# Scales of MLP weights from a 2-norm on ScalarE, halves of an exponential buffer split, two modulation steps a period instead of three: a two-layer diffusion backbone on one core

## The chip, the cores and the metric

One Trainium2 chip, one of its cores. The time is device microseconds of one execution; the kernel before took 2903.8 us in the median of 3 runs (2901.84 to 2909.9). The kernel is written with a tile framework: the program names tiles and operations, and a planner that works with an estimated timeline sets semaphores, buffers and the order of each engine's queue at compile time. On the chip every engine works through its queue in that order.

## The reference, cut to what matters

```python
for layer in range(2):
    mp, ms = ada_mod(c_ctx, w_ada[layer], b_ada[layer]), ada_mod(c, w_ada[layer], b_ada[layer])
    h = modulate(rmsnorm(x, norm1[layer]), m[0], m[1])
    # layer 0: mixer A (windowed attention with sink) and mixer B (differential attention); layer 1: RG-LRU
    x = x + m[2] * mixer(h)
    h = modulate(rmsnorm(x, norm2[layer]), m[3], m[4])
    x = x + m[5] * (square(relu(h @ w_mlp1[layer])) @ w_mlp2[layer])
y = rmsnorm(x, final_norm)

# ada_mod: silu(c) @ w + b, split in six; w is 1024 x 6144
# diff_attention: w = softmax(q1 k1 * SCALE) - lam * softmax(q2 k2 * SCALE); w @ v
```

There are 1,024 latent and 128 context tokens, width 1,024, an MLP width of 4,096, and everything is fp32.

## The kernel before, in words

TensorE works on fp16 pairs. Each fp32 operand becomes hi + lo after multiplication by a power of two, and a product is three matmuls. The power of two comes from a bound of the operand: it has to be large enough for precision and small enough that nothing overflows.

**The MLP** (`mlp`, L474). The weights come in quarters of 1,024 KB (class `Quad`, L2103): 16 upper ones (kind U, 256 columns of w_mlp1) and 16 lower ones (kind D, 512 x 512 of w_mlp2) a layer, 64 in all, in two staging buffers `st` of 128x2048. The products go by a scheme with seven block products in place of eight, so a quarter is split twice: as it is, then after sums of its blocks. A quarter goes through these steps, spread over the products of the two quarters before it (`pieces` in `mlp`):

- `load`: a DMA from SP's queue into `st`;
- `peak` (L2113): VectorE takes the largest absolute value of each partition (`rowmax`, L109, or the reduction at L2120 for the two halves of a lower quarter, each with its own scale), TensorE spreads these over the partitions (`across`, L115: a matmul with the column repeated as weights and the identity as the moving operand), and VectorE takes the maximum again (L123);
- `bits` (L2123): VectorE makes the scale in one-column instructions (`pow2s`, L94 to L103, and others);
- `prepare`: ScalarE writes hi (L2142) and VectorE lo (L2143), in halves of 128x1024; GpSimd forms the block sums in place (L2163 to L2166); hi and lo again. After the last lo the staging buffer is free for the next load.

Meanwhile ScalarE applies relu and square (L650, L651) to the upper products, GpSimd and VectorE form sums of the activations (L639 to L642, L569), ScalarE and VectorE or GpSimd split these (L151, L152), and VectorE adds finished lower products to X (L713). The products (L520) turn through six PSUM accumulators; TensorE starts one when VectorE or ScalarE has emptied it. The prompt's 128 tokens have small tiles of their own: `gt` (two buffers, fp32 128x256) for its activations.

**The attention** (`attention`, L871). Units of mixer A and of mixer B, 36 each, are started, exponentiated, combined, split, transposed by DMA and multiplied with V. What a unit does when is written in tables of offsets in periods (`PLAN_A`, `PLAN_B`, `PLAN_C` for the last nine units of mixer B); all events are sorted by these due times, and the program is written out in that order, from period -9 to 39. In mixer B a unit has two score matrices of 128x1152. `peak` (L1201) scales a matrix out of PSUM with its maximum, `exps` (L1208) exponentiates it in place with its sum, and `combine` (L1215) subtracts the second from the first. Both halves lie in one tile `S` of 128x2304 with two buffers; the first half is then read by ScalarE (L1076) and GpSimd (L1080).

Beside the units the projections' products run in slices, and the remaining modulation (class `Ada`, L2003): five thirds of a w_ada, each 16 loads of 512 KB (L2019) into `sa` (two buffers), 16 steps of four matmuls (L2036), and three steps that copy, turn and add. An event `adas` loads one piece ahead and makes one step; `PLAN_ADA` says at which offsets of each period it stands.

```python
def adas():
    if len(ada.loaded) < (1 if ada.turning else 2):
        ada.load()
    ada.step()
...
for o in PLAN_ADA:
    events.append((p + o, adas))
```

Of the kernel before, what the change touches and what calls it, by code (L numbers as in the profile page):

```python
# [7 lines left out]
F32 = mybir.dt.float32  # L8
F16 = mybir.dt.float16
BF16 = mybir.dt.bfloat16  # L10
I32 = mybir.dt.int32
AF = mybir.ActivationFunctionType
ALU = mybir.AluOpType
AX = mybir.AxisListType.X
# [3 lines left out]
P = 128  # L18
# [4 lines left out]
NT = LAT + CTX  # L23
# [15 lines left out]
PLAN_SLICE = (0.999, 0.975, 0.65, 0.196, 0.452, 0.974)  # L39
PLAN_TAIL = (0.062, 0.261, 0.999)  # L40
PLAN_PREP = (0.728, 0.074, 0.477)
PLAN_ADA = (0.08, 0.583, 0.749)
STB = 6
STEP = "sc G0 L x wp s0 x G1 rw x wa s1 G2 s2 x gp ex pr x G3 x ga gb s3 x x te wb sq p0 e0 cs xs yh e1 wh R cv yo gs wo i1 i0 U p1"
GATES = ((0, 0), (1, 0), (0, 1), (1, 1))
# [7 lines left out]
class Net:  # L53
# [61 lines left out]
    def across(self, out, t):  # L115


        n = t.shape[1]
        o = 512 - n * P
        ps = self.bank(0)[:, o:]  # L120
        for i in range(n):
            self.nc.tensor.matmul(ps[:, i * P:(i + 1) * P], t[:, i:i + 1].to_broadcast([P, P]), self.ident, start=True, stop=True)
        self.nc.vector.tensor_reduce(out, ps.rearrange("p (n c) -> p n c", n=n), axis=AX, op=ALU.max)  # L123

    def rsqrt_guess(self, y, v, n):
        self.nc.gpsimd.tensor_tensor(y, v, self.mhalf[:, :n], op=ALU.pow)
# [347 lines left out]
    def mlp(self, l, X, np_, R, finish, ahead, after):  # L474
# [6 lines left out]
        nc = self.nc  # L481
        v = nc.vector
        w1, w2 = self.a["w_mlp1"][l], self.a["w_mlp2"][l]
        A, B, z, gate = np_
# [15 lines left out]
        def bits(it):  # L500
            kind, i, c = it
            w = Ws[it]
            if it != seq[0]:
                w.bits(None if kind == "U" else [y[:, 2 * i + j, 4:5] for j in range(2)])
            if kind == "U":

                o = y[:, i]
                v.tensor_scalar(o[:, 0:1], w.q[:, 2:3], z[:, 2:3], 32.0, op0=ALU.mult, op1=ALU.mult)
                self.pow2(o[:, 2:4], o[:, 0:1], 7)
                v.tensor_scalar(o[:, 1:2], o[:, 2:3], z[:, 1:2], w.q[:, 1:2], op0=ALU.mult, op1=ALU.mult)  # L510
                v.tensor_scalar(o[:, 4:5], o[:, 3:4], o[:, 3:4], None, op0=ALU.mult)
            else:
                gc = gcs[i, c] = self.sm.tile([P, 4, 2], F32, tag="gc", name="gc", bufs=4)
                nc.scalar.activation(gc, gate[:, 4 * c:4 * c + 4, :], AF.Copy, scale=w.q[:, 1:2])
# [287 lines left out]
        for n, it in enumerate(seq):  # L802
            todo = pieces(n)
            kind, i, c = it
# [66 lines left out]
    def attention(self, np_, es):  # L871


        nc, a, tc = self.nc, self.a, self.tc
        v = nc.vector
        A, B, z, gate = np_
# [4 lines left out]
        late = es.enter_context(tc.tile_pool(name="a3", bufs=2))  # L881
# [24 lines left out]
        res = {}  # L906
# [109 lines left out]
        def piece(which=("tail", "prep")):  # L1016
            for w in which:
                next(work[w], None)
# [89 lines left out]
        class UnitA(Unit):  # L1108
# [39 lines left out]
            def exps(u):  # L1148
                st = u.st
                for x in range(2):  # L1150
                    nc.scalar.activation(u.S[:, x], u.S[:, x], AF.Exp, bias=st[:, 2 + x:3 + x], accum_out=st[:, 6 + x:7 + x])
                    nc.scalar.activation(st[:, 4 + x:5 + x], sink[:, 2 * u.j + x:2 * u.j + x + 1], AF.Exp, bias=st[:, 2 + x:3 + x])

            def whole(u):
                return u.S.rearrange("p x n -> p (x n)")
# [21 lines left out]
        class UnitB(Unit):  # L1177
# [17 lines left out]

            def peak(u, x):
                if x == 0:
                    u.S = late.tile([P, 2 * NT], F32, tag="S", name="S")[:, :2 * u.nk].rearrange("p (x n) -> p x n", x=2)
                    u.st = late.tile([P, 10], F32, tag="stB", name="stB", bufs=5)
                st = u.st  # L1200
                v.tensor_scalar(u.S[:, x], u.ps[:, :u.nk], res["cs", "qb", u.h], None, op0=ALU.mult, op1=ALU.max, accum_out=st[:, x:x + 1])  # L1201
                if x == 0:
                    v.tensor_scalar(st[:, 2:3], st[:, 0:1], -1.0, ln_c, op0=ALU.mult, op1=ALU.add)
                else:
                    v.tensor_scalar(st[:, 3:4], st[:, 1:2], -1.0, None, op0=ALU.mult)

            def exps(u, x):
                nc.scalar.activation(u.S[:, x], u.S[:, x], AF.Exp, bias=u.st[:, 2 + x:3 + x], accum_out=u.st[:, 4 + x:5 + x])  # L1208

            def combine(u):  # L1210

                S, st = u.S, u.st
                v.reciprocal(st[:, 6:7], st[:, 5:6])
                v.tensor_scalar(st[:, 7:8], st[:, 6:7], st[:, 4:5], neg_lam, op0=ALU.mult, op1=ALU.mult)
                v.scalar_tensor_tensor(S[:, 0], S[:, 1], st[:, 7:8], S[:, 0], op0=ALU.mult, op1=ALU.add)  # L1215

            def whole(u):
                return u.S[:, 0]

            def norm(u):  # L1220
                st = u.st
# [114 lines left out]
        for us, first, table in ((ua, -9, PLAN_A), (ub, 0, PLAN_B)):  # L1336
            for i, u in enumerate(us):
# [8 lines left out]
                t = -1e9  # L1346
                if us is ub and i >= 27:
                    table = PLAN_C
                for k, o in table:
                    t = max(t + 1e-4, first + i + o)  # L1350
                    if k in fs:
                        events.append((t, fs[k]))
        for p in range(-9, 36 + 4):
# [4 lines left out]
            for o in PLAN_PREP:  # L1358
                events.append((p + o, lambda: piece(("prep",))))
            for o in PLAN_ADA:  # L1360
                events.append((p + o, adas))
# [398 lines left out]
    def run(self):  # L1760
        nc, a, tc, ctx = self.nc, self.a, self.tc, self.ctx
        v = nc.vector
# [5 lines left out]
        with tc.tile_pool(name="rows", bufs=1, side="right") as rp:  # L1768
            self.setup(rp)
            with ExitStack() as es, tc.tile_pool(name="xt", bufs=1, side="right") as xp, tc.tile_pool(name="xu", bufs=3, side="right") as tp:  # L1770
# [25 lines left out]
                for blk in range(4):  # L1796
                    g = block(blk)
# [43 lines left out]
        self.stg, self.wp, self.wsize = wa_set  # L1841
        with tc.tile_pool(name="X0", bufs=1) as xp, ExitStack() as es:
            X = xp.tile([P, KD, NT], F32, tag="X", name="X")
            buf = Bufs()
            buf.first(es.enter_context(tc.tile_pool(name="ra0", bufs=1)))
            buf.second(es.enter_context(tc.tile_pool(name="rb0", bufs=1)))
            sq = [buf("f0"), buf("f1"), buf("f2")[:, :P]]
            rst2 = self.rstd_cols("b")
            o = self.new_h(0)
            oc = [self.h_chunk(o, c) for c in range(3)]  # L1850
            for k in range(KD):
                for c, (c0, c1) in enumerate(CH):
                    nc.sync.dma_start(out=oc[c][k], in_=oD[k, :, :, c0:c1])
            w_out = a["att_w_out"][0]

            def entry(m):
                self.stg, self.wp, self.wsize = wa_set if m < 2 else wm_set
                hi, lo, q = self.wcols(w_out, m * P, P)
                nc.sync.dma_start(out=X[:, m], in_=xD[m])
                gc = self.sm.tile([P, 2], F32, tag="gco", name="gco", bufs=8)  # L1860
                v.tensor_scalar(gc, np1[3][:, m, :], q[:, 1:2], inv_o, op0=ALU.mult, op1=ALU.mult)
                return m, [(hi[:, k], lo[:, k]) for k in range(KD)], o, gc

            plan = [lambda m=m: entry(m) for m in range(KD)]


            def ahead():
                wa.close()
                buf.third(es.enter_context(tc.tile_pool(name="rt0", bufs=1)))
                self.mlp_first(0)  # L1870

            u = buf.ring(*KEEP)
            self.residual(X, plan, lambda m: X[:, m], sq, rst2, buf.ring("f3", "f4", "f5"), ahead,
                          self.normed(X, rst2, np2, [u, u, buf.ring("gt")], True))
            rst3 = self.rstd_cols("c")
            tps = ctx.enter_context(tc.tile_pool(name="taps", bufs=5, side="right"))
            tmp = buf.ring("T3_0", "T3_1", "T3_2", "T3_3", "T4_0", "T4_1")
            sqs = []

            def finish(c, m, i):  # L1880
                if not sqs:
                    sqs.extend([buf("T2_0"), buf("T2_1"), buf("T2_2")[:, :P]])
                self.finish_chunk(X, sqs, rst3, c, m, tmp, i)

            nps = []

            def ahead(c):
                if c == 0:
                    nps.extend([self.norm_params(1, 1), self.norm_params(1, 2), self.recurrent(nps, tps, xD2)])
                else:  # L1890
                    next(nps[2])

            self.mlp(0, X, np2, buf, finish, ahead, self.normed(X, rst3, nps, tmp))
            np4, rec = nps[1:]
            for k in range(KD):
                nc.sync.dma_start(out=xD2[k], in_=X[:, k])
# [2 lines left out]
        plan, xk = rec.send(yp)  # L1899
        with tc.tile_pool(name="X1", bufs=1) as xp, ExitStack() as es:  # L1900
            X = xp.tile([P, KD, NT], F32, tag="X", name="X")
            buf = Bufs()
            buf.first(es.enter_context(tc.tile_pool(name="ra1", bufs=1)))
            hk = lambda k, c: self.hk.tile([P, CH[c][1] - CH[c][0]], F32, tag=f"hk{k}_{c}", name=f"hk{k}_{c}")
            sq = [hk(7, c) for c in range(3)]
# [11 lines left out]
            u = buf.ring(*KEEP)  # L1917
# [141 lines left out]
class Chunk:  # L2059
# [19 lines left out]
    def peak(self):  # L2079
        self.rows()  # L2080
        self.over()
# [21 lines left out]
class Quad(Chunk):  # L2103
# [9 lines left out]
    def peak(self):  # L2113
        n = self.net
        self.q = n.sm.tile([P, 6], F32, tag="wq", name="wq", bufs=8)
        if self.up:
            n.absmax(self.q[:, 2:3], self.st)
        else:
            t = n.small(2, "am")
            n.nc.vector.tensor_reduce(t, self.st.rearrange("p (t c) -> p t c", t=2), axis=AX, op=ALU.max, apply_absolute_value=True)  # L2120
            n.across(self.q[:, 2:4], t)

    def bits(self, inv=None):  # L2123

# [117 lines left out]
```

## Time and profile before

| | |
|---|---|
| median of 3 runs | 2903.8 us |
| the profiled execution | 2898.73 us |
| its span | 2896.9 us |
| granted TensorE clock, mean | 0.942 |
| TensorE busy | 2530.9 us (87%) |
| VectorE busy | 2135.3 us (74%) |
| ScalarE busy | 1409.2 us (49%) |
| GpSimd busy | 1275.1 us (44%) |

PE is TensorE, PEld its weight loads, DVE is VectorE, ACT ScalarE, POOL GpSimd, SP SyncE, whose queue issues the DMAs. A name such as `am<-st` says which tile an instruction writes and reads, and L112 is a line of the kernel. A wait is idle time of an engine, under the name of what ended it. Setup lasts to about 60 us, the attention to about 700 us, the first MLP from about 820 to 1,560 us, the recurrent mixer to about 2,000 us, and the second MLP from about 2,110 us to the end.

### The profile page before, as it was taken

To read this page: it belongs to the slowest core of one execution; us is meant where nothing else is said; L and a number is where in the kernel's file an instruction comes from. 1 tells how busy PE (TensorE), PEld (TensorE's weight loads), DVE (VectorE), ACT (ScalarE), POOL (GpSimd) and SP (SyncE) were. 2 spreads that over 40 slices of the span, in tenths; PEclk is the share of its full clock that TensorE was granted. 3 is DMA by queue.
4 is the path that set the end of the run, shared out by engine and by line. 5 is a ranking of instruction groups with operands and counts; after the bars stand their busy time and mean duration, and the time that the engine had idled before them with its cause. 6 is when DMAs were issued, how large, how long until landed. Compare 5 with 4: busy or idle time off the path is not lost. (4 is left out here: it accounts for less than half of the span.)

```text
span 2896.9 us, 44653 instructions
## 1 busy us (share of the span) xinstructions
PE 2530.9 (87%) x17572; PEld 1391.7 (48%) x17572; DVE 2135.3 (74%) x4208; ACT 1409.2 (49%) x2177; POOL 1275.1 (44%) x978
## 2 busy tenths in 40 slices
PE   7889888867969999999997988878969999999998
PEld 3555545644534445444553444434535455444555
DVE  5556666774698777887789588786488778777786
ACT  4345666762254444444444567773244444344443
POOL 1445554631255444354435244454255444444434
PEclk8999999988979999999998999998979999999999
DMA  8598997764101111111112011112101111111101
GB/s 299 154 219 207 208 207 188 159 125 141 52 15 59 44 45 44 59 45 43 46 44 109 27 65 65 46 49 86 44 2 62 42 57 45 44 49 39 57 32 66
DMA packets 296964, 245.46 MB, mean 85 GB/s; under 512 B 152195, under 2 KB 254258, under 8 KB 296626
## 3 DMA queue, kind: packets, MB, share of 16 engines
q1 hardware_dynamic: 296754, 242.62, 30.2%
q8 instruction: 137, 2.24, 0.3%
q14 instruction: 73, 0.60, 0.1%
HBM read 176.38 MB, written 19.54 MB: 68 GB/s over the span
## 5 line engine op out<-in xcount | busy, mean ns | idle before, releaser
L520 PEld LDWEIGHTS <-hi 128*128 128x128 f16 x5456 | 490.9, 98 | 477.9 <-issue 82.1
L520 PE MATMUL ps<-g,hi 128*128 128x512 f16 x1792 | 539.0, 385 | 59.7 <-DVE X L713 31.8
L197 PE MATMUL ps<-hk,hi 128*128 128x512 f16 (+1 forms) x2160 | 463.7, 340 | 64.1 <-DVE hk L365 40.9
L2142 ACT ACTIVATE hi<-st,wq 128x1024 f16<-128x1024 f32 x252 | 277.9, 1139 | 314.0 <-POOL st L2165 139.0
L2143 DVE SCALAR_TENSOR_TENSOR lo<-st,wq,hi 128x1024 f16<-128x1024 f32 x252 | 343.1, 1371 | 97.0 <-ACT hi L2142 95.9
L520 PEld LDWEIGHTS <-lo 128*128 128x128 f16 x2728 | 268.3, 98 | 232.6 <-DVE lo L2143 19.4
L520 PE MATMUL ps<-hk,hi 128*128 128x512 f16 (+1 forms) x1920 | 375.1, 301 | 3.4 <-ACT hi L2142 3.2
L197 PEld LDWEIGHTS <-hi 128*128 128x128 f16 x2640 | 236.7, 102 | 256.1 <-issue 62.3
L520 PE MATMUL ps<-g,lo 128*128 128x512 f16 x896 | 340.1, 385 | 9.2 <-DVE lo L2143 9.2
L197 PE MATMUL ps<-hk,lo 128*128 128x512 f16 (+1 forms) x1080 | 269.8, 336 | 0.4 <-DVE lo L2094 0.4
L520 PE MATMUL ps<-hk,lo 128*128 128x512 f16 (+1 forms) x960 | 263.5, 301 | 1.5 <-DVE my L97 1.4
L713 DVE SCALAR_TENSOR_TENSOR X<-ps,gc,X 128x128 f32<-128x128 f32 (+1 forms) x416 | 244.4, 619 | 5.1 <-PE ps L520 5.0
L2163 POOL TENSOR_TENSOR st<-st 128x256 f32<-128x256 f32 (+1 forms) x94 | 104.1, 1120 | 282.5 <-DVE lo L2143 275.9
L112 DVE TENSOR_REDUCE am<-st 128x1 f32<-128x2048 f32 (+1 forms) x71 | 135.8, 1921 | 110.9 <-DMA st<-in_w_mlp_dram 61.6
L520 PE MATMUL ps<-T,hi 128*128 128x512 f16 x720 | 215.1, 381 | 2.7 <-DVE f L569 2.7
L151 ACT ACTIVATE g<-f 128x512 f16<-128x512 f32 x224 | 138.1, 623 | 162.6 <-PE ps L520 93.3
L197 PEld LDWEIGHTS <-lo 128*128 128x128 f16 x1320 | 119.1, 101 | 154.1 <-issue 56.4
L152 DVE TENSOR_TENSOR g<-f,g 128x512 f16<-128x512 f32 x134 | 123.4, 923 | 73.2 <-ACT g L151 73.2
L152 POOL TENSOR_TENSOR g<-f,g 128x512 f16<-128x512 f32 x90 | 123.5, 1377 | 114.2 <-ACT g L151 114.1
L639 POOL TENSOR_TENSOR f<-f,f 128x512 f32<-128x512 f32 x30 | 38.2, 1273 | 246.3 <-ACT f L651 240.5
L569 DVE TENSOR_TENSOR f<-ps,f 128x512 f32<-128x512 f32 x190 | 129.5, 684 | 11.9 <-PE ps L520 6.4
L650 ACT ACTIVATE f<-f,my 128x512 f32<-128x512 f32 x90 | 64.7, 719 | 151.3 <-DVE f L569 151.1
(480 smaller groups left out, 4961.6 us busy)
## 6 DMA issues: line engine op xcount, KB each, us to landing
st<-in_w_mlp_dram SPq DMA_DIRECT2D x64, 1024.0 KB, 5.4
sa<-in_w_ada_dram SPq DMA_DIRECT2D x80, 512.0 KB, 4.5
st<-in_rec_w_in_dram SPq DMA_DIRECT2D x10, 1024.0 KB, 5.0
st<-in_w_ada_dram SPq DMA_DIRECT2D x16, 512.0 KB, 7.2
st<-in_att_w_in_dram SPq DMA_DIRECT2D x16, 512.0 KB
X<-xD SPq DMA_DIRECT2D x14, 576.0 KB, 9.4
kb<-HL SPq DMA_DIRECT2D x16, 320.0 KB, 6.8
st<-in_rec_w_out_dram SPq DMA_DIRECT2D x5, 1024.0 KB, 4.9
```

The costliest lines, as they stand in the source:

```text
L112: self.nc.vector.tensor_reduce(t, src, axis=AX, op=ALU.max, apply_absolute_value=True)
L151: nc.scalar.activation(hi, src, AF.Copy)
L152: (eng or nc.vector).tensor_tensor(lo, src, hi, op=ALU.subtract)
L197: nc.tensor.matmul(out[:, a:b], w[wi], h[hj][:, a:b], start=start and p == 0, stop=stop and p == 2)
L520: nc.tensor.matmul(ps, ws[k][a], hs[k][b], start=first and k == 0 and i == 0, stop=last and k == n - 1 and i == 2, skip_group_check=not (f ...
L569: v.tensor_tensor(to, st[a], st[b], op=ALU.add)
L639: e.tensor_tensor(t1, c12, c11, op=ALU.subtract)
L650: nc.scalar.activation(dst, src, AF.Relu, scale=sc)
L713: v.scalar_tensor_tensor(X_, t_, gc[:, m, STREAM[cc]:STREAM[cc] + 1], X_, op0=ALU.mult, op1=ALU.add)
L2142: n.nc.scalar.activation(v[0][:, c], self.st[:, c], AF.Copy, scale=sc)
L2143: n.nc.vector.scalar_tensor_tensor(v[1][:, c], self.st[:, c], sc, v[0][:, c], op0=ALU.mult, op1=ALU.subtract)
L2163: e.tensor_tensor(b(1, 1), b(1, 0), b(1, 1), op=ALU.add)
```

## The change

Three edits. `Quad.peak` takes the scale's bound from a 2-norm of the weights: ScalarE squares a quarter in four pieces of 128x512 with a sum for each partition, its other output going to a `gt` buffer; `root_sum` sums over the partitions with four matmuls of one column, whose weights are the repeated columns of sums; and VectorE approximates the root by a shift and an addition on the bits. `bits` in `mlp` loses the factor 32 in the upper quarters' bound, since the 2-norm bounds the product without it. The first and second half of mixer B's `S` become tiles `S0` with three buffers and `S1` with one. `PLAN_ADA` loses its third offset.

```diff
-PLAN_ADA = (0.08, 0.583, 0.749)
+PLAN_ADA = (0.08, 0.583)
...
+    def root_sum(self, out, t, groups):
+        v = self.nc.vector
+        n, g = out.shape[1], groups
+        ps = self.bank(0)[:, 512 - n:]
+        for i in range(n):
+            for k in range(g):
+                self.nc.tensor.matmul(ps[:, i:i + 1], t[:, i * g + k:i * g + k + 1].to_broadcast([P, P]), self.ones[:, 0:1], start=k == 0, stop=k == g - 1)
+        v.tensor_scalar(out, ps, 1e-24, 3e38, op0=ALU.max, op1=ALU.min)
+        oi = out.bitcast(I32)
+        v.tensor_scalar(oi, oi, 1, None, op0=ALU.logical_shift_right)
+        v.tensor_scalar(oi, oi, float(0x1FC20000), None, op0=ALU.add)
...
-                v.tensor_scalar(o[:, 0:1], w.q[:, 2:3], z[:, 2:3], 32.0, op0=ALU.mult, op1=ALU.mult)
+                v.tensor_scalar(o[:, 0:1], w.q[:, 2:3], z[:, 2:3], None, op0=ALU.mult)
...
                 if x == 0:
-                    u.S = late.tile([P, 2 * NT], F32, tag="S", name="S")[:, :2 * u.nk].rearrange("p (x n) -> p x n", x=2)
+                    u.S = []
...
+                u.S.append(late.tile([P, NT], F32, tag=f"S{x}", name=f"S{x}", bufs=3 - 2 * x)[:, :u.nk])
+                v.tensor_scalar(u.S[x], u.ps[:, :u.nk], res["cs", "qb", u.h], None, op0=ALU.mult, op1=ALU.max, accum_out=st[:, x:x + 1])
...
-        if self.up:
-            n.absmax(self.q[:, 2:3], self.st)
-        else:
-            t = n.small(2, "am")
-            n.nc.vector.tensor_reduce(t, self.st.rearrange("p (t c) -> p t c", t=2), axis=AX, op=ALU.max, apply_absolute_value=True)
-            n.across(self.q[:, 2:4], t)
+        t = n.small(4, "am")
+        for i in range(4):
+            n.nc.scalar.activation(n.buf("gt").bitcast(BF16), self.st[:, 512 * i:512 * i + 512], AF.Square, accum_out=t[:, i:i + 1])
+        n.root_sum(self.q[:, 2:3] if self.up else self.q[:, 2:4], t, 4 if self.up else 2)
```

`exps`, `combine` and `whole` use `u.S[x]` where they used `u.S[:, x]`, and the program keeps `buf` as `self.buf`.

## Rows read from the trace of the kernel before

**Rows 1.** Stretches: length, busy us of PE, PEld, DVE, ACT, POOL, PEclk, DMA share, GB/s.
```profile
60.00:510.00 450.00, 384.51 (x4011) 235.37 (x4009) 288.80 (x961) 249.65 (x537) 229.83 (x145) 0.94 0.82 193
510.00:700.00 190.00, 132.06 (x1276) 91.59 (x1275) 125.14 (x397) 112.26 (x258) 71.35 (x45) 0.84 0.68 150
860.00:1530.00 670.00, 636.07 (x4018) 335.76 (x4017) 529.52 (x893) 297.75 (x425) 309.36 (x285) 0.99 0.15 48
2161.00:2861.00 700.00, 663.52 (x4169) 349.13 (x4168) 555.54 (x915) 311.01 (x447) 327.95 (x301) 0.99 0.14 44
2485.40:2488.90 3.50, 3.50 (x9) 1.23 (x9) 3.50 (x7) 0.63 (x1) 2.74 (x3) 0.51 0.00 0
```
**Rows 2.** Waits of TensorE over the span: us in total, times, longest us.
```profile
PE ps L2036 <- DMA sa<-in_w_ada_dram: 41.0, 27, 4.5
...
PE ps L520 <- DVE X L713: 36.2, 17, 3.6
...
PE ps L520 <- ACT hi L2142: 13.3, 10, 2.2
...
PE ps L520 <- DVE lo L2143: 9.8, 15, 0.7
```
**Rows 3.** Timeline of DVE, second MLP: start us, us, instruction, [idle before].
```profile
2480.53 2.29 DVE L112 TENSOR_REDUCE am<-st 128x1 f32<-128x2048 f32 x1 [2.50 <-DMA st<-in_w_mlp_dram]
2482.73 1.27 DVE L2143 SCALAR_TENSOR_TENSOR lo<-st,wq,hi 128x1024 f16<-128x1024 f32 x1
2483.93 0.68 DVE L569 TENSOR_TENSOR f<-ps,f 128x512 f32<-128x512 f32 x1
2484.53 0.74 DVE L713 SCALAR_TENSOR_TENSOR X<-ps,gc,X 128x512 f32<-128x512 f32 x1
...
2491.76 0.28 DVE L123 TENSOR_REDUCE wq<-ps 128x1 f32<-128x128 f32 x1
2492.07 0.15 DVE L94 TENSOR_SCALAR wq<-wq 128x1 f32<-128x1 f32 x1
```
**Rows 4.** Timeline of PE, second MLP: the stop, and the next one.
```profile
2482.12 0.38 PE L520 MATMUL ps<-g,lo 128*128 128x512 f16 x1
2485.32 0.91 PE L520 MATMUL ps<-g,hi 128*128 128x512 f16 x2 [2.82 <-DVE X L713]
...
2576.71 0.59 PE L520 MATMUL ps<-g,hi 128*128 128x512 f16 x2 [3.55 <-DVE X L713]
```
**Rows 5.** Waits of DVE over the span, for the landings of MLP weights.
```profile
DVE am L112 <- DMA st<-in_w_mlp_dram: 61.6, 23, 5.5
...
DVE am L2120 <- DMA st<-in_w_mlp_dram: 41.6, 27, 3.3
```
**Rows 6.** Timeline of PE, second MLP: a maximum across partitions, the product after it.
```profile
2490.89 0.38 PE L122 MATMUL ps<-ident,am 128*128 128x128 f32 x2
2491.11 0.59 PE L520 MATMUL ps<-g,hi 128*128 128x512 f16 x2
```
**Rows 7.** Timeline of PE after the attention: sums of squares, the product after them.
```profile
775.56 0.95 PE L413 MATMUL ps<-ones,f 128*128 128x1 f32 x8
776.37 0.38 PE L197 MATMUL ps<-hk,hi 128*128 128x512 f16 x1
```
**Rows 8.** Groups of ACT (busy us, mean ns | idle before); last, its timeline.
```profile
L2142 ACT ACTIVATE hi<-st,wq 128x1024 f16<-128x1024 f32 x252 | 277.9, 1139 | 314.0 <-POOL st L2165 139.0 <-POOL st L2166 125.0 <-PE ps L520 42.2
...
L651 ACT ACTIVATE f<-f 128x512 f32<-128x512 f32 x128 | 79.9, 627 | 3.0
...
L1151 ACT ACTIVATION_READ_ACCUMULATOR SA<-SA,stA 128x1 f32 x72 | 13.6, 189 | 0.0
...
2454.70 2.17 ACT L2142 ACTIVATE hi<-st,wq 128x1024 f16<-128x1024 f32 x2
```
**Rows 9.** Busy time of L2036 from 60 to 700 us; landing of its loads.
```profile
sum 640.00, PE 58.43 PEld 14.69; mean PE 8.35 PEld 2.10
...
DMA to landing us min/median/max: 3.6/4.5/6.0
```
**Rows 10.** Mixer B's tile S: a wait, and durations ns min/median/max.
```profile
DVE S L1201 <- POOL W L1080: 6.9, 4, 2.8
...
L1208 ACT ACTIVATE S<-S,stB x72: 384/1247/1267, 208.0 to 653.0; 128x1152 f32<-128x1152 f32 x64, 128x128 f32<-128x128 f32 x8
...
L1215 DVE SCALAR_TENSOR_TENSOR S<-S,stB x36: 341/1418/3482, 214.0 to 654.1; 128x1152 f32<-128x1152 f32 x32, 128x128 f32<-128x128 f32 x4
```

More of the change, by code (lines that the diff above doesn't have):

```diff
@@ L1197, in peak @@
                 if x == 0:
-                    u.S = late.tile([P, 2 * NT], F32, tag="S", name="S")[:, :2 * u.nk].rearrange("p (x n) -> p x n", x=2)
+                    u.S = []
                     u.st = late.tile([P, 10], F32, tag="stB", name="stB", bufs=5)
                 st = u.st
-                v.tensor_scalar(u.S[:, x], u.ps[:, :u.nk], res["cs", "qb", u.h], None, op0=ALU.mult, op1=ALU.max, accum_out=st[:, x:x + 1])
+                u.S.append(late.tile([P, NT], F32, tag=f"S{x}", name=f"S{x}", bufs=3 - 2 * x)[:, :u.nk])
+                v.tensor_scalar(u.S[x], u.ps[:, :u.nk], res["cs", "qb", u.h], None, op0=ALU.mult, op1=ALU.max, accum_out=st[:, x:x + 1])
                 if x == 0:
@@ L1207, in exps @@
             def exps(u, x):
-                nc.scalar.activation(u.S[:, x], u.S[:, x], AF.Exp, bias=u.st[:, 2 + x:3 + x], accum_out=u.st[:, 4 + x:5 + x])
+                nc.scalar.activation(u.S[x], u.S[x], AF.Exp, bias=u.st[:, 2 + x:3 + x], accum_out=u.st[:, 4 + x:5 + x])
             def combine(u):
@@ L1214, in combine @@
                 v.tensor_scalar(st[:, 7:8], st[:, 6:7], st[:, 4:5], neg_lam, op0=ALU.mult, op1=ALU.mult)
-                v.scalar_tensor_tensor(S[:, 0], S[:, 1], st[:, 7:8], S[:, 0], op0=ALU.mult, op1=ALU.add)
+                v.scalar_tensor_tensor(S[0], S[1], st[:, 7:8], S[0], op0=ALU.mult, op1=ALU.add)
             def whole(u):
-                return u.S[:, 0]
+                return u.S[0]
             def norm(u):
@@ L1843, in run @@
             X = xp.tile([P, KD, NT], F32, tag="X", name="X")
-            buf = Bufs()
+            buf = self.buf = Bufs()
             buf.first(es.enter_context(tc.tile_pool(name="ra0", bufs=1)))
@@ L1901, in run @@
             X = xp.tile([P, KD, NT], F32, tag="X", name="X")
-            buf = Bufs()
+            buf = self.buf = Bufs()
             buf.first(es.enter_context(tc.tile_pool(name="ra1", bufs=1)))
```

## The prediction

> **What bounds the kernel now.** I began with the split of time by stretch, to see which engine is full where, and went from there to the list of what TensorE waits for, then to the order of time around one such wait.
>
> The stretches [rows 1] show three parts that the change touches. The two MLPs (860 to 1530 us and 2161 to 2861 us) have TensorE busy for 636 of 670 us and 664 of 700, VectorE for 79%, ScalarE for 44%, and a granted clock of 0.99. The attention up to 510 us has TensorE busy for 385 of 450 us, the clock at 0.94, and the DMA engines 82% busy; after 510 us TensorE is busy for only 132 of 190 us. So TensorE is the limit, and what can be won is its waits, its half-clock time, and work taken off it.
>
> The waits of TensorE [rows 2] name four causes of interest: the MLP's accumulators that VectorE has not emptied yet (X, 36.2 us in 17 waits), MLP weights not split yet (hi 13.3 us, lo 9.8 us), and the modulation weights still in flight (41.0 us in 27 waits).
>
> The order of time around one of the 17 [rows 3] tells why VectorE is late. It stands idle for 2.50 us in front of a maximum whose weights have not landed, takes 2.29 us for the maximum, then 1.27 us for a split, and only then empties two accumulators. TensorE stops 2.82 us [rows 4] and restarts slower: from 2485.40 to 2488.90 the clock is 0.51, the lower of the two levels, 1.2 of 2.4 GHz [rows 1]. The next such stop ends at 2576.71 us [rows 4], 91 us later, which is a period of four weight loads; the MLPs have about 15 of these. VectorE's waits for these landings are 61.6 and 41.6 us over the span [rows 5].
>
> **MLP scales: VectorE and TensorE's waits.** 64 reductions of 2.29 us (147 us) and up to 103 us of waiting leave VectorE's queue [rows 3, 5]. In their place come three one-column instructions, for the one reduction across partitions that also goes; Three of some 0.15 us replace one of 0.28 [rows 3]; I cost this at nothing, since VectorE keeps a fifth of its time free, and without that cover it would be some 0.2 us a quarter, 13 us. What comes back is TensorE's wait for X: of 36.2 us I take 33, because the row shows it is the 4.8 us in front of the accumulators that makes them late. Half-clock time in both MLPs is 1% of 1,370 us, 13.7 us [rows 1]; the low clock follows the stop, so I take 10 back. Bounds: 0 (VectorE is then held by its other work) to 50. What is late next are the weights, hi and lo.
>
> **MLP scales: TensorE's added work.** Before, one maximum across partitions moves 128 columns: from 2490.89 to the next product at 2491.11, 0.22 us, and twice that for the lower weights with two scales [rows 6]. Now every quarter has four matmuls of one column, each with its own 128x128 fp32 weights. The same shape stands in the trace as the sums of squares: eight records (four matmuls) from 775.56 to the next product at 776.37, 0.81 us [rows 7]. So 32 x (0.81 - 0.22) + 32 x (0.81 - 0.44) = 18.9 + 11.8 = 31 us more on the full engine. Part hides where TensorE would have waited for weights anyway (13.3 + 9.8 us); I take 5 of it. Bounds: 8 us (all 23 us of those waits filled) and 44 us (a quarter of the 64 cases at the lower clock, where 0.81 us doubles).
>
> **MLP scales: ScalarE's added work.** A square of 128x512 takes 0.627 us and an accumulator read 0.189 [rows 8], so a quarter costs 4 x 0.816 = 3.3 us, 209 us for 64. ScalarE has 56% of the MLP free, and its largest idle times are in front of the split of hi, for GpSimd's sums (139.0 and 125.0 us, [rows 8]). I cost this at nothing: the square now stands idle for the landing where VectorE did, and behind it wait the splits of hi, which wait for GpSimd today. If that cover is gone a switch of quarters is 3.3 us late; this is the rival below. The squares' output goes to the two buffers of the prompt's activations; ScalarE writes both, and VectorE's read of the prompt's is short, so nothing is queued behind it. The factor of 32 that goes removes no instruction.
>
> The row says the move is from 2.29 us of one engine to 3.3 us of another. The Trainium skill, ScalarE: Activation LUTs, section "Rules for kernel authors", says that multiplications and maxima belong on VectorE, not ScalarE, as VectorE does them faster. By that rule the change loses time; the trace agrees on the price of one, and the sum differs because VectorE's queue is the one TensorE waits for here.
>
> MLP in sum: -33 - 10 + 31 - 5 = -17 us.
>
> **Modulation steps, three to two a period.** 95 steps in 98 places (49 periods of two): five thirds of 16 matmul steps and 3 turning steps. They now last to the attention's end instead of 510 us. All 80 loads stay, on SP's queue, later and between the transposes and K/Q copies of that queue. A load lands 4.5 us after its issue (3.6 to 6.0, [rows 9]), and steps two calls apart at offsets 0.583 and 0.749 leave 0.17 of a period, 2.2 us (640 us from 60 to 700 us over 49 periods: 13 us). With two calls it is 6.5 us, longer than the longest landing. So of the 41.0 us of waits I take 31. The lost clock before 510 us is 6% of 450, 27 us [rows 1]; a third follows these waits, 9 us. From the 40 I keep three quarters, 30, because VectorE (64%) and ScalarE (55%) with their PSUM turnarounds are late next. The matmuls take 58.4 us of TensorE [rows 9]; a third, 19.5, moves behind 510 us, where TensorE has 58 us idle. The front gets two thirds of that back (-13), the rear pays half (+10), and five more waits of about a us for landings there make +5. Sum -28 us. Bounds: 0 (other engines take it all) and -80 (41 + 19 of clock + 20 moved).
>
> **Halves of mixer B's exponentials.** VectorE waited 6.9 us in 4 cases for GpSimd to leave the old whole buffer [rows 10]; a third buffer for the first half ends these. The second half now has one buffer: in the last nine units its next maximum must wait for exponentials (1.25 us) and the combination (1.42 us) of the unit before [rows 10]. In a period of some 10 us that fits, because VectorE's order puts the combination first. I take 0; bounds -7 and 9 x 2.7 = +24.
>
> **Sum.** -17 - 28 + 0 = -45 us. The profiled execution took 2898.7 us around a span of 2896.9; it stands 5.1 us below the median of the runs, 2903.8. I set the sum against the median: 2859 us, and 2854 for a profile. About 0.3%, 9 us, is what a measurement of this kernel can tell from no change.
>
> **Rivals.**
> - *Attention gives nothing.* Steps still come to TensorE in close pairs, or the time moves to VectorE's accumulators. For it: up to 510 us VectorE is busy for 289 of 450 us and ScalarE for 250 [rows 1], both with PSUM that TensorE waits to write. Against: 41.0 us of waits are on TensorE itself [rows 2]. 2904 - 17 = 2887 us. This is also the case in which the change only half does what it says. Chance 0.22.
> - *All waits close.* The weights' waits (23 us) go with the accumulators', and attention comes near its bound: MLP -36 - 14 - 19 + 31 = -38, attention -60; 2806 us. For it: VectorE is also in the chain of the weights' lo. Chance 0.14.
> - *ScalarE becomes late: slower.* The squares stand in ScalarE's queue ahead of the next splits of hi, so hi, GpSimd's sums and the second split of each of the two lower quarters a period come 3.3 us later to TensorE. Price 2 x 15 x 3.3 = 98 us: 2904 + 98 - 45 = 2957 us. It decides from the point where ScalarE's idle time between a landing and the next split of hi is under 3.3 us. For it: the lower quarters' splits run as soon as their scales exist, two in 2.17 us at 2454.70 [rows 8]. Against: the VectorE delay of 4.8 us in the same chain goes at the same time. The rule of the skill named above would lead here. Chance 0.14.
>
> **How the numbers follow.** The forecast has 0.50, with a range of its own from 2825 to 2885 us. Of the 0.22 for attention giving nothing, 0.06 fall within 9 us of the median; of the 0.14 for ScalarE, 0.02. Faster: 0.50 + 0.16 + 0.14 = 0.80; same: 0.08; slower: 0.12. The range from 2805 to 2895 us takes in the forecast, most of the first rival and half of the second, and leaves out about 0.2.
>
> **What would show it.** Right: TensorE's waits for X in the MLP under 10 us in all, a clock of 1.00 there, VectorE's share down by about 10 points and ScalarE's up by 14; the four small matmuls at about 0.8 us; waits for the modulation weights near 10 us, with steps up to the end of the attention. Wrong: TensorE waiting for ScalarE's hi or for the sums of squares by tens of us in the MLP; waits for modulation weights as long as before; VectorE waiting for the second half's buffer; an attention as long as before although those waits are gone.

## The result, and the profile after

The changed kernel took 2851.5 us in the median of 4 runs (2850.2 to 2857.5) beside 2904.6 us for the kernel before: a ratio of 0.982 with a 95% interval of 0.980 to 0.984, some 52 us faster. The forecast was 2859 us, 45 us faster. The sum is right by luck: two of its terms are far off and cancel, as the MLPs gave 48 us where 17 were forecast, and the attention nothing where 28 were.

The page of the changed kernel, span and busy time of each engine:

```profile
span 2849.9 us, 45942 instructions
...
PE 2553.0 (90%) x17892; PEld 1428.4 (50%) x17892; DVE 2024.3 (71%) x4272; ACT 1564.7 (55%) x2689; POOL 1287.3 (45%) x978
```

TensorE is busy for 2,553 us in a span of 2,850: what is left to win is the 297 us in which it is idle, and the work itself.

Stretches of the changed kernel, with the columns of [rows 1]: the attention before and after 510 us, the first MLP over the same 670 us, and the second.

```profile
60.00:510.00 450.00, 394.27 (x3972) 241.82 (x3971) 298.36 (x986) 260.55 (x557) 240.66 (x150) 0.94 0.77 178
510.00:700.00 190.00, 129.22 (x1317) 85.73 (x1318) 122.28 (x376) 103.93 (x239) 66.28 (x39) 0.85 0.77 187
860.00:1530.00 670.00, 662.08 (x4269) 359.86 (x4267) 505.60 (x970) 379.27 (x676) 322.68 (x293) 1.00 0.16 53
2140.00:2816.00 676.00, 671.69 (x4325) 364.44 (x4324) 508.28 (x961) 382.24 (x683) 331.91 (x301) 1.00 0.14 46
```

In the MLPs TensorE now has work for 99% of the time at a clock of 1.00, where it had 95% at 0.99 [rows 1]; VectorE went from 79% to 75%, where the prediction's sign was about 10 points, and ScalarE from 44% to 57%. The attention looks as it did, but for a DMA share that is lower in front and higher behind.

TensorE's waits over the span: us, times, longest. The first line is of the kernel before, for sums of activations (f) that [rows 2] leave out; the others are of the changed kernel, where L534 is the line of the MLP's products and L2052 that of the modulation's matmuls.

```profile
PE ps L520 <- DVE f L569: 16.8, 18, 4.2
...
PE ps L2052 <- DMA sa<-in_w_ada_dram: 37.6, 22, 4.9
...
PE ps L534 <- DVE f L583: 7.8, 5, 4.8
...
PE ps L534 <- DVE X L727: 2.1, 5, 0.7
...
PE ps L534 <- ACT hi L2157: 0.9, 2, 0.5
```

The waits for X fell from 36.2 us to 2.1, and those for hi and lo (13.3 and 9.8 us, [rows 2]) to 0.9 us and none; those for the sums f fell from 16.8 to 7.8 us. The modulation's stand at 37.6 us after 41.0. By marks in the two traces, the first accumulation of the layer's output projection, which follows the attention, comes at 673.0 us after 673.3. From there to the first MLP's last product it is 868 us after 894, and from the recurrent layer's last such accumulation to the second MLP's last product 740 after 762: 48 us together. The recurrent mixer between has 413 us after 412.

### The profile page after: what moved, and what is told of

Its sections match the earlier page's. It is cut to its first block, busy times and chain, and to the rows that moved or that the text cites. A ratio compares the mean times of both kernels' runs of the same rounds, so it can differ in the third digit from the quotient of the medians.

```text
span 2849.9 us, 45942 instructions
## 1 busy us (share of the span) xinstructions
PE 2553.0 (90%) x17892; PEld 1428.4 (50%) x17892; DVE 2024.3 (71%) x4272; ACT 1564.7 (55%) x2689; POOL 1287.3 (45%) x978
## 3 DMA queue, kind: packets, MB, share of 16 engines
q8 instruction: 140, 2.29, 0.3%
## 5 line engine op out<-in xcount | busy, mean ns | idle before, releaser
L534 PEld LDWEIGHTS <-hi 128*128 128x128 f16 x5456 | 493.8, 99 | 414.5 <-issue 24.7
L534 PE MATMUL ps<-g,hi 128*128 128x512 f16 x1792 | 534.8, 380 | 12.7 <-DVE f L583 7.8
L2158 DVE SCALAR_TENSOR_TENSOR lo<-st,wq,hi 128x1024 f16<-128x1024 f32 x252 | 357.5, 1427 | 166.2 <-ACT hi L2157 165.9
L534 PE MATMUL ps<-hk,hi 128*128 128x512 f16 (+1 forms) x1920 | 374.0, 301 | 0.9 <-ACT hi L2157 0.9
L534 PEld LDWEIGHTS <-lo 128*128 128x128 f16 x2728 | 267.7, 98 | 208.4 <-issue 3.8
L534 PE MATMUL ps<-g,lo 128*128 128x512 f16 x896 | 337.6, 380 | 0.0
L2178 POOL TENSOR_TENSOR st<-st 128x256 f32<-128x256 f32 (+1 forms) x94 | 96.0, 1035 | 382.1 <-DVE lo L2158 377.0
L534 PE MATMUL ps<-hk,lo 128*128 128x512 f16 (+1 forms) x960 | 263.5, 301 | 0.1
L2135 ACT ACTIVATE gt<-st 128x512 bf16<-128x512 f32 x256 | 158.6, 620 | 126.5 <-DMA st<-in_w_mlp_dram 122.6
L534 PE MATMUL ps<-T,hi 128*128 128x512 f16 x720 | 214.0, 379 | 0.0
L211 PEld LDWEIGHTS <-lo 128*128 128x128 f16 x1320 | 118.5, 101 | 166.0 <-issue 61.6
L166 POOL TENSOR_TENSOR g<-f,g 128x512 f16<-128x512 f32 x90 | 131.2, 1463 | 58.3 <-ACT g L165 58.3
L166 DVE TENSOR_TENSOR g<-f,g 128x512 f16<-128x512 f32 x134 | 115.2, 860 | 46.8 <-ACT g L165 46.8
L534 PE MATMUL ps<-T,lo 128*128 128x512 f16 x360 | 136.1, 379 | 0.0
```

Source lines behind the costliest of these rows:

```text
L166: (eng or nc.vector).tensor_tensor(lo, src, hi, op=ALU.subtract)
L211: nc.tensor.matmul(out[:, a:b], w[wi], h[hj][:, a:b], start=start and p == 0, stop=stop and p == 2)
L534: nc.tensor.matmul(ps, ws[k][a], hs[k][b], start=first and k == 0 and i == 0, stop=last and k == n - 1 and i == 2, skip_group_check=not (f ...
L2135: n.nc.scalar.activation(n.buf("gt").bitcast(BF16), self.st[:, 512 * i:512 * i + 512], AF.Square, accum_out=t[:, i:i + 1])
L2158: n.nc.vector.scalar_tensor_tensor(v[1][:, c], self.st[:, c], sc, v[0][:, c], op0=ALU.mult, op1=ALU.subtract)
L2178: e.tensor_tensor(b(1, 1), b(1, 0), b(1, 1), op=ALU.add)
```

## Experiments

Theory A throughout was that TensorE is full in the MLPs and lost time to VectorE's queue, and that the attention edits changed nothing that it waits for. Ratios are to the kernel before on the same chip, with 95% intervals; the changed kernel's is 0.982.

**The three edits one by one.** The first has the new `root_sum` and `peak` alone, the second this line, the third the tiles `S0` and `S1`:

```diff
-PLAN_ADA = (0.08, 0.583, 0.749)
+PLAN_ADA = (0.08, 0.583)
```

> The kernel before with the MLP scales' edit alone (sums of squares, four one-column matmuls); three modulation steps a period and the whole S buffer stay. Theory A (all of the gain is the MLP's): 48 us faster than before, about 2856 us, with the attention's stretch as before and under 15 us of TensorE's waits in either MLP. Theory B (the prediction's split, 17 us from the MLP and 28 from the attention): about 2888 us.

Measured: 2854.6 us beside 2897.6, 0.985 (0.983 to 0.987), 43 us faster. TensorE waited 1.7 us for X in all. The split of the prediction falls: the MLP edit alone gives over four fifths of the gain.

> The kernel before with two modulation steps a period alone. Theory A (TensorE's waits for the modulation weights stay, since a load is issued only 4 to 6 us ahead of its step whatever the number of steps): within 6 us of before, waits for these weights of 35 to 40 us. Theory B (the prediction): 28 us faster, waits near 10 us. Theory C (two steps gain and the split halves lose it again): 10 to 20 us faster.

Measured: 2893.0 beside 2897.6, 0.9987 (0.9973 to 1.0001): 4 us, just not told from nothing. The waits for the modulation weights were 39.9 us in 23 cases. The prediction's 28 us fall, and so does a gain that the halves would hide.

> The kernel before with mixer B's halves in own buffers alone. Theory A: within 6 us of before, VectorE's 7 us of waits for GpSimd gone and none for the one buffer of the second half in their place. Theory C (the one buffer holds up the last nine units and hides a gain of the two modulation steps): 10 to 24 us slower.

Measured: 2887.6 beside 2897.6, 0.9965 (0.9953 to 0.9978): 10 us faster, which no theory named. VectorE's 7 us of waits for GpSimd are gone as expected, but the attention ends only 1 us sooner in its trace (672.1 us). 8 of the trace's 14 us lie between the first MLP's last product and the recurrent mixer's first scan, 90 us in place of 98, which the edit doesn't touch. The order of several instructions is another there, and one wait went. That wait before:

```profile
PE ps L122 <- DVE am L112: 6.4, 1, 6.4
```

and in the run with the halves:

```profile
PE ps L122 <- DVE am L112: 0.7, 1, 0.7
```

Two more kernels ask whether any edit that makes the planner write another order does that.

```diff
-PLAN_ADA = (0.08, 0.583, 0.749)
+PLAN_ADA = (0.08, 0.583, 0.74)
```

> The kernel before with the third modulation offset at 0.74 in place of 0.749, which moves a few instructions in the planner's order and changes no work. Theory A (the 10 us of the split halves come from the planner ordering far-off code anew): a time that also differs from before by some us, up to 10 either way, with the difference in parts that the edit doesn't touch. Theory B (the halves themselves gave the 10 us): within 3 us of before.

Measured: 2899.8 beside 2899.5, 0.9996 (0.9983 to 1.0009). No shift of 10 us.

```diff
-                    u.S = late.tile([P, 2 * NT], F32, tag="S", name="S")[:, :2 * u.nk].rearrange("p (x n) -> p x n", x=2)
+                    u.S = []
...
+                u.S.append(late.tile([P, NT], F32, tag=f"S{x}", name=f"S{x}", bufs=2)[:, :u.nk])
```

> The kernel before with mixer B's halves in own buffers, two of each, so that there are as many buffers as before and only the tiles are finer. Theory A (the third buffer of the first half gave the 10 us): within 4 us of before. Theory B (any change of these tiles that makes the planner write another order gives a few us either way): a time away from before by 4 to 12 us, with the difference outside the attention.

Measured: 2904.9 beside 2902.7, 1.0003 (0.9993 to 1.0013). So finer tiles give nothing, and three and one buffers do give 10 us by themselves. In both of these traces the order of instructions in the stretch from the first MLP to the first scan is that of before, apart from its edges; in the run with three and one buffers it is another for TensorE, VectorE and GpSimd. So these two kernels do not show what any other order there would give, and how the third buffer changed it is open. In the changed kernel the same stretch has no such gain: the recurrent mixer's 413 us are those of before.

**VectorE's queue or something else?** The pass over a quarter goes back to VectorE, all else stays as changed:

```diff
-        for i in range(4):
-            n.nc.scalar.activation(n.buf("gt").bitcast(BF16), self.st[:, 512 * i:512 * i + 512], AF.Square, accum_out=t[:, i:i + 1])
+        n.nc.vector.tensor_reduce(t, self.st.rearrange("p (t c) -> p t c", t=4), axis=AX, op=ALU.max, apply_absolute_value=True)
```

> The changed kernel with the pass over a quarter back on VectorE: one reduction of 128x2048 to four columns (a maximum in place of sums of squares, so the scales come from other numbers); the four one-column matmuls, the instructions on the bits and the attention stay as changed. Theory A (VectorE's queue behind a landing made TensorE wait): the waits for X in the MLPs come back, 30 to 45 us in all, the clock falls to 0.98 to 0.99, and with 31 us of added matmuls the time is 2905 to 2935 us, slower than both. Theory D (the gain lies elsewhere, in the shorter work on the scales): 2850 to 2870 us.

Measured: 2921.1 beside 2897.6, 1.008 (1.005 to 1.010), slower than both kernels. TensorE's waits in the MLPs came back, spread over more causes than X:

```profile
PE ps L534 <- DVE f L583: 22.5, 23, 2.5
PE ps L534 <- DVE X L727: 19.8, 15, 1.8
PE ps L534 <- DVE Y L557: 18.5, 10, 2.1
...
PE ps L534 <- ACT hi L2156: 1.2, 2, 0.7
...
PE ps L534 <- DVE lo L2157: 0.4, 1, 0.4
```

The first three are tiles that VectorE writes. The waits for hi and lo did not come back, although VectorE also writes lo. Against the changed kernel the run is some 74 us slower, for one instruction of 2.29 us a quarter on another engine. Theory A holds in the time; X alone, at 19.8 us, came below its 30 to 45.

**Is TensorE full, and what do the four matmuls cost?** In the changed kernel one sum over the partitions stands so in TensorE's timeline:

```profile
2529.82 0.38 PE L534 MATMUL ps<-hk,lo 128*128 128x512 f16 x1
2530.04 0.95 PE L133 MATMUL ps<-ones,am 128*128 128x1 f32 x8
2530.85 0.59 PE L534 MATMUL ps<-g,hi 128*128 128x512 f16 x2
```

From 2530.04 to the next product it is 0.81 us, as in [rows 7]. Now ones are the weights and the four columns move:

```diff
-        ps = self.bank(0)[:, 512 - n:]
-        for i in range(n):
-            for k in range(g):
-                self.nc.tensor.matmul(ps[:, i:i + 1], t[:, i * g + k:i * g + k + 1].to_broadcast([P, P]), self.ones[:, 0:1], start=k == 0, stop=k == g - 1)
-        v.tensor_scalar(out, ps, 1e-24, 3e38, op0=ALU.max, op1=ALU.min)
+        ps = self.bank(0)[:, 512 - n * g:]
+        self.nc.tensor.matmul(ps, self.ones[:, 0:1].to_broadcast([P, P]), t, start=True, stop=True)
+        v.tensor_reduce(out, ps.rearrange("p (n g) -> p n g", n=n), axis=AX, op=ALU.add)
+        v.tensor_scalar(out, out, 1e-24, 3e38, op0=ALU.max, op1=ALU.min)
```

> The changed kernel with another sum over the partitions: the weights are a repeated column of ones and the four columns of sums move, one matmul of four columns in place of four of one; VectorE adds the columns with one more small reduction. Theory A (TensorE is full in the MLPs, so its work there counts whole): each sum falls from 0.81 to about 0.2 us, 64 x 0.6 = 38 us less, 30 to 38 us faster than the changed kernel, 2813 to 2821 us. Theory B (weights come late next): the waits for hi and lo come back by as much and the time falls by under 10 us.

Measured: 2805.2 beside 2896.5, 0.967 (0.964 to 0.970). That is 0.015 of 2,900, 44 us, below the changed kernel's ratio, and more than theory A's 30 to 38. Its sum over the partitions:

```profile
2408.87 0.28 PE L131 MATMUL ps<-am,ones 128*128 128x4 f32 x2
2409.01 0.59 PE L533 MATMUL ps<-g,hi 128*128 128x512 f16 x2
...
PE ps L533 <- ACT hi L2156: 8.5, 3, 3.8
```

It is 0.14 us to the next product. 64 x (0.81 - 0.14) = 43 us were taken from TensorE, and about all of them came back as time: in the changed MLPs TensorE's work counts whole. Waits for hi came to 8.5 us in 3 cases, a fifth of that gain at most.

**Is ScalarE near its limit?** Every square twice:

```diff
-        for i in range(4):
+        for i in (0, 1, 2, 3, 0, 1, 2, 3):
```

> The changed kernel with every square taken twice, the second in place of the first: 209 us more on ScalarE, 3.3 us a quarter. Theory A (ScalarE has room in the MLPs): its share there goes from 0.56 to about 0.7 and the time rises by under 15 us. Theory B (the prediction's slower rival: ScalarE's splits become late): 60 to 100 us slower than the changed kernel, with TensorE waiting for hi.

Measured: 2862.7 us, 0.988 (0.985 to 0.990), 15 us over the changed kernel, at the edge of theory A. ScalarE's busy time rose by 149 us over the span, from 1,564.7, and not by the 209 of the expectation; in the first MLP's 670 us it went from 379 to 447 us. The page's line and TensorE's waits:

```profile
PE 2552.0 (89%) x17892; PEld 1425.5 (50%) x17892; DVE 2010.3 (70%) x4272; ACT 1713.7 (60%) x3201; POOL 1279.3 (45%) x978
...
PE ps L534 <- DVE X L727: 6.7, 17, 0.8
PE ps L534 <- ACT hi L2157: 6.5, 2, 3.3
...
PE ps L133 <- ACT gt L2135: 5.5, 4, 2.5
```

TensorE waits for hi in 2 cases and for the squares themselves in 4, of 64 quarters. The slower rival had 98 us for 3.3 us more on ScalarE a quarter; the 2.3 us a quarter that were added here cost 15.

**The waits for the modulation weights.** In the changed kernel the SP queue and TensorE, in order of time, at one of the 22:

```profile
404.25 1.05 PE L2052 MATMUL ps<-sa,sc 128*32 128x256 f32 x10
404.95 1.96 SPq L1077 DMA_TRANSPOSE WT<-W  x1
407.00 0.99 SPq L1120 DMA_DIRECT2D oD<-ot  x1
408.09 1.22 SPq L1023 DMA_DIRECT2D qb<-HL  x2
408.79 0.63 PE L2052 MATMUL ps<-sa,sc 128*32 128x256 f32 x6
409.40 0.54 SPq L2035 DMA_DIRECT2D sa<-in_w_ada_dram  x1
410.53 3.76 SPq L1077 DMA_TRANSPOSE WT<-W  x1
...
413.80 0.87 PE L2052 MATMUL ps<-sa,sc 128*32 128x256 f32 x8 [4.38 <-DMA sa<-in_w_ada_dram]
```

The step comes 4.4 us behind its load's issue, and a load of this kind takes 5.0 us to land in this kernel's page. A step is eight records here, so the row at 404.25 holds one whole step and the start of the next. The two buffers are filled in turn (many loads are issued 0.06 us after the end of the step two before them), so this load's buffer was free when the step at 404.25 had ended, at 404.9 us; the load was issued 4.5 us later, behind a transpose, a store and two copies in SP's queue. Over the trace, 13 of the 22 waits, 28 of the 37.6 us, stand behind loads that were issued 2.7 us or more after their buffer was free, each with a transpose (L1077) before it in SP's queue. So most of these leads are short by what stands in that queue, and others because a step frees the buffer late; no run here puts the loads ahead of the transposes. Is the lead too short because the load stands too late in the program?

```diff
         ada.load()
+        ada.load()
...
-            if len(ada.loaded) < (1 if ada.turning else 2):
-                ada.load()
             ada.step()
+            if len(ada.loaded) < (1 if ada.turning else 2):
+                ada.load()
```

> The changed kernel with each modulation event's step written ahead of its load and one more load before the first, so that a load stands a whole event earlier with the same two buffers. Theory A (these waits stand in for others: the order of the units sets the attention's length): the 37.6 us of waits fall to under 10 us and the attention's end moves by less than 8 us. Theory B (the prediction: such waits are lost one for one): 25 to 35 us faster than the changed kernel.

Measured: 2848.7 us, 0.983 (0.980 to 0.985), as the changed kernel, but with 41.2 us of these waits in 28 cases. Neither theory could be tried by it, since the edit did not move the loads on the chip: from a load's issue to its step it is 6.5 us in the median in both traces.

> The changed kernel with one load for all of the attention's modulation steps: 79 loads of 512 KB (40 MB) are left out, and the steps multiply with the first one's weights, so the modulation's numbers are not the reference's. Theory A: no waits for these weights, DMA share before 510 us down from 0.77 to about 0.5, the attention's end within 10 us of the changed kernel's 673 us. Theory B: the attention ends 30 to 40 us sooner.

Its edit: the first load stays, later ones only name the same tile again.

```diff
-        def sa():
-            return late.tile([P, 1024], F32, tag="sa", name="sa", bufs=2)
+        kept = late.tile([P, 1024], F32, tag="sa", name="sa", bufs=1)
...
-            self.last = self.net.loads.dma_start(out=st, in_=self.net.a["w_ada"][l][k * P:(k + 1) * P, c:c + 1024])
+            if not (self.once and self.loads_made):
+                self.last = self.net.loads.dma_start(out=st, in_=self.net.a["w_ada"][l][k * P:(k + 1) * P, c:c + 1024])
+            self.loads_made = True
```

Measured in a single execution: 2821.4 us, without any interval; the attention ends at 645.2 us, 28 sooner. That stretch:

```profile
60.00:645.00 585.00, 487.88 (x5196) 324.90 (x5194) 405.58 (x1336) 356.27 (x789) 305.85 (x189) 0.92 0.57 116
```

TensorE, VectorE and ScalarE are busy for 83%, 69% and 61% of it: none of the three is full even now. So the waits, the loads and what hangs on them cost some 28 us together, about what the prediction put on the waits. Some of it is taken by the units' own waits: before and after, TensorE waited for the scores' buffers (S) 14 us in the changed kernel and 32 in this one. The steps were all done by 341 us, in the changed kernel by 608, so the written order puts them much earlier when no load stands before them. That shift is in the 28 us too, and the run does not part it from the waits.

Last, three buffers, at the price of one for `S0`:

```diff
-            return late.tile([P, 1024], F32, tag="sa", name="sa", bufs=2)
-
-        ada = Ada(self, self.ada_todo, 1, sa, lambda: late.tile([P, 512], F32, tag="sa", name="at", bufs=2))
+            return late.tile([P, 1024], F32, tag="sa", name="sa", bufs=3)
+
+        ada = Ada(self, self.ada_todo, 1, sa, lambda: late.tile([P, 512], F32, tag="sa", name="at", bufs=3))
+        ada.load()
         ada.load()
...
-            if len(ada.loaded) < (1 if ada.turning else 2):
+            if len(ada.loaded) < (2 if ada.turning else 3):
...
-                u.S.append(late.tile([P, NT], F32, tag=f"S{x}", name=f"S{x}", bufs=3 - 2 * x)[:, :u.nk])
+                u.S.append(late.tile([P, NT], F32, tag=f"S{x}", name=f"S{x}", bufs=2 - x)[:, :u.nk])
```

> The changed kernel with three buffers for the modulation weights and one load more ahead, paid for by two buffers in place of three for the first half S0. Theory A (the wait comes from two buffers: a load waits for the step that frees its buffer, and the next step comes 4 to 6 us behind): the 37.6 us of waits fall to under 15 us and the attention ends 10 to 28 us sooner. Theory B (the planner places steps as soon as it believes a load landed, however many buffers): 30 to 45 us of waits and an attention of the same length.

Measured: 2828.4 beside 2899.5, 0.9755 (0.974 to 0.977), some 19 us below the changed kernel. Its attention ends at 650.3 us, 23 sooner, with these waits:

```profile
PE ps L2053 <- DMA sa<-in_w_ada_dram: 23.3, 17, 2.6
```

14 us of waits fewer, not the 23 or more that were expected, but 23 us of the time. The steps are done by 511 us here, by 608 in the changed kernel and by 509 in the one before: with a third buffer they went back to the front, so that the 23 us, too, hold both fewer waits and earlier steps, and the run does not part them. It also shows that the third buffer of `S0` is not needed for an attention of this length.

> The weights of ones and the three buffers together. Theory A: the two gains add, 2777 to 2795 us. Theory B (three buffers give nothing): 2800 to 2810 us.

Measured: 2791.5 beside 2899.5, 0.962 (0.961 to 0.964). The gains of the weights of ones and of the three modulation buffers add within the noise, and the version beats both kernels: 108 us below before. Its page:

```profile
span 2791.7 us, 45213 instructions
...
PE 2494.5 (89%) x17508; PEld 1384.6 (50%) x17508; DVE 2004.6 (72%) x4336; ACT 1567.2 (56%) x2689; POOL 1264.7 (45%) x978
```

Beside the changed kernel's, the busy time of TensorE has fallen by 58.5 us, that of the other three by less than 25 each, where it fell, and the span by 58.2.

## Why the prediction was right, and where it was not

**VectorE's queue and the wait for X** (33 of 36.2 us forecast): 34 came back. The mechanism is the one named; the run with the pass on VectorE shows it from the other side. What was mis-sized is what lies beside it. The prediction said "What is late next are the weights, hi and lo" and let the added matmuls fill 5 of these 23 us; 22 went, and so did 9 of the 17 us for f, which it had left out. For f the cause is VectorE's queue: with the pass back on VectorE these waits came to 22.5 us. For hi and lo it is not shown. They stayed away in that run (1.2 and 0.4 us), although VectorE stood behind the landings again, and ScalarE writes hi [rows 2]. That run keeps the added matmuls, and with the cheap ones 8.5 us for hi came back, so part of it can be the prediction's own bound, "all 23 us of those waits filled".

**TensorE's added work** (31 us): the price was right, 0.81 us a quarter in the row shown. What of it hid (5 us) cannot be told apart from the weights' waits that went. **The clock** (10 us back): 0.99 to 1.00 over 1,370 us, about 14 by the rounded figures. An account after the fact, with the waits in full: -34 - 22 - 9 + 31 - 14 = -48 us, against 48 by the marks and 43 for the edit alone. Forecast -17. So close a sum does not show that each term is right.

**ScalarE** (nothing): right. The ScalarE queue now waits for the landing:

```profile
L2135 ACT ACTIVATE gt<-st 128x512 bf16<-128x512 f32 x256 | 158.6, 620 | 126.5 <-DMA st<-in_w_mlp_dram 122.6 <-DVE gp L674 3.9
L2135 ACT ACTIVATION_READ_ACCUMULATOR gt<-st 128x1 f32 x256 | 48.6, 190 | 0.0
```

The idle time behind loads, 61.6 + 41.6 us on VectorE [rows 5], became 122.6 us on ScalarE, and it costs next to nothing there: TensorE waits 0.9 us for hi and 1.3 us for the squares. The durations in the two rows come to 207 us for 209 forecast, but they overlap: ScalarE's busy time rose from 1,409.2 to 1,564.7 us, by 156. So a quarter takes some 2.4 us of ScalarE and not 3.3; adding the durations of a square and of its read was the wrong reading. The Trainium skill, ScalarE: Activation LUTs, section "Rules for kernel authors", would keep such work on VectorE. In the trace the price of one quarter is about the same, 2.4 us in place of 2.29, and on the kernel the trace disagrees: 43 us faster, since the engine that gave up the work was the one TensorE waited for.

**Modulation steps** (-28 us): 4 us alone, nothing seen in the changed trace. The step that failed is "with two calls it is 6.5 us, longer than the longest landing". The offsets give the order of the program, and the order on the engines is another: in the changed trace a step stands at 404.2 us, the next begins 0.5 us later, at 404.7, and ends at 409.4, and the one after it, behind a wait of 4.38 us, comes at 413.8. Its load had been issued 4.4 us ahead, held by what stood before it in SP's queue. The waits near 10 us that the prediction gave as a sign stayed at 37.6.

Of the three terms, that the waits would go was wrong; their price stays open, as a kernel without the loads ends its attention 28 us and one with three buffers 23 us sooner, but both also have their steps earlier. Of the steps a fifth moved behind 510 us (12.7 of 63.9 us of TensorE's busy time), not a third. The forecast of 13 us for the front and 10 back in the rear is not borne out either. By the 27th of mixer B's combinations, before the last nine units, the changed kernel is 12 us ahead and in the end 2 (577.4 us after 589.5, 652.3 after 654.1), which looks like it; but with the modulation edit alone the 27th came 1 us sooner and the last 1 us later (588.4, 654.9). The 27th before, changed, and with that edit alone:

```profile
589.49 0.43 DVE L1215 SCALAR_TENSOR_TENSOR S<-S,stB 128x128 f32<-128x128 f32 x1
...
577.39 0.35 DVE L1231 SCALAR_TENSOR_TENSOR S<-S,stB,S 128x128 f32<-128x128 f32 x1
...
588.40 0.35 DVE L1215 SCALAR_TENSOR_TENSOR S<-S,stB 128x128 f32<-128x128 f32 x1
```

**Halves** (nothing): 10 us faster alone, outside the forecast's bounds of -7 to +24, in a part that the edit does not touch. Nothing of the second half's one buffer is seen: VectorE has no wait for it in the changed kernel, where the combination that frees it is VectorE's own.

Of the rivals, "attention gives nothing" was right for the attention and "all waits close" for the MLPs. The chance of 0.50 belonged to a split between the two that did not occur as described; its time did.

## What to carry to other kernels

A wait for a landing belongs in the queue of an engine that the full engine hardly waits for: here 103 us of idle time and 147 us of work left VectorE, 123 and 156 us came to ScalarE, and the kernel gained 43 us. Read for each row of the full engine's waits which engine writes the tile; rows with the same writer can go and come together, as X and f did, but lo did not come back with them. Take what an instruction costs from an engine's busy time or from one start to the next, as durations in a queue overlap. When an engine is full, count its small instructions too: one operand order of the same little sum costs 0.81 us and the other 0.14, and over 64 of them that was 43 us. An offset in a plan is not a time on the chip: look at the step, at the issue of its load and at what stands before the load in its queue before a gain is counted on it. A third buffer helped here (23 us of the attention); another order of the queue was not tried.

## What the runs showed that was not expected

The third buffer of `S0` and the single one of `S1` moved 8 us in a stretch 900 us later, where the same instructions run in another order, while two buffers of each, and an offset moved by 0.009, left that order alone and moved nothing that can be measured. And three modulation buffers took 14 us from TensorE's waits by name but 23 us from the attention, with the steps done 97 us sooner, so a wait's own row need not be the whole of what an edit gives back.
